# One transformer block after another on one core: which instructions rank first on three engines, and the recurrence's functions ordered by kind

## The chip, the cores and the metric

The kernel runs on one core of a Trainium2 chip. A core has a tensor engine (TensorE, PE in the profile) that multiplies 128 x 128 weights with up to 512 columns and writes to PSUM, a vector engine (DVE), a scalar engine with table functions (ACT), GpSimd (POOL, which here reads and writes SBUF only), and a sync engine (SP) that only issues transfers here. Each engine works off its own queue in order, and a semaphore holds an instruction back until its inputs are there. The metric is the device time in microseconds (us): 2860.61 is the median of three runs (2860.28 to 2860.99).

## The reference

512 tokens of width 1024, fp32, go through two blocks.

The first block (depth 1): a hybrid mixer (dilated attention of 8 heads and a retention of 4 heads on the normalised input, joined by an output projection), cross attention to 256 memory tokens (4 heads), and a SwiGLU feed-forward with 2816 hidden columns. Each of the three is added as `x + rms_norm(y)`.

The second block (depth 2), each layer: half a SwiGLU feed-forward, a mixer, half a SwiGLU feed-forward, each with a shift, a scale and a gate worked out from a conditioning vector `c` by a 1024 x 9216 matrix. Its mixer joins a gated linear recurrence on 512 channels, stick-breaking attention (4 heads) and forgetting attention (4 heads):

```
r, i  = sigmoid(u @ w_r + b_r), sigmoid(u @ w_i + b_i)
a     = exp(-8 * r * softplus(-lam))
h_t   = a_t * h_(t-1) + sqrt(1 - a_t^2) * i_t * u_t
y_lru = h * gelu(lru_g)
y     = concat(rms(y_lru), rms(y_sb), rms(y_fox)) * g_mix_out
x     = x + gate * (y @ w_out)
```

## The kernel before, in words

**Matrix products.** Every large product runs as three products of split numbers (`mm3`, L367 to L373): an fp32 weight tile of 128 x 1024 is loaded by SP (`weights`, L339, three raw buffers), ACT casts it to the upper half (L348), DVE, or in a few places POOL, subtracts to get the lower half (L350), with six buffers for each half. Activations are kept as such pairs too. The token axis of 512 is the column axis.

**Stage ends.** A stage that ends in a norm is cut into two halves of 256 tokens (`slab4` with `halves`, L431). For each of 8 row tiles and each half, DVE adds the PSUM result into X (`end_plain`, L571) or into Y (`end_post`, L599), ACT squares it and POOL sums the squares (`square_sum`, L514 to L524). A product with ones sums over partitions (`cols`, L485), `rsqrt` (L472) scales on DVE (L475) and takes the power -0.5 on POOL (L476), and `spread` turns the result back into a row for all partitions (L508). From that, DVE, ACT and POOL make the next activations (`norm_half`, L540 to L561). In the first block, `end_post` with `apart` squares and sums the new X as well (L628). The weights for the next stage are loaded and split beforehand (L451 to L453).

**The feed-forward** (`ffn`, L666) works in three slabs of 9, 9 and 4 hidden tiles, gate and up first and then down; the end of the third slab is the stage end above.

**The conditioning products** (`ada`, L837): 144 rows, each a 512 KB transfer through the raw buffers and one DVE multiply-and-sum (L849). While `calm` is true, each call of `weights` adds 0.7 row to what is due (L341); stage ends set `calm` to false, the first gate-up products to true (L400). `modulated(n)` calls for what is still missing.

**The second block's mixer** (`mixer2`, L1393): q and k of the stick-breaking heads; then values by tokens (`keep`, L1620), copied out of PSUM by ACT and DVE in turn (`copy`, L334); q and k of the forgetting heads (`qk`, L1419); then the recurrence's inputs (`lru_in`, L1633). Meanwhile the heads run as streams: scores, exponentials, turning the probabilities over TensorE into PSUM (`flip`), a copy to SBUF (`turn`, L1503), and the product with the values (`weigh`, L1508). `lru` (L1325) holds the recurrence: tanh for the gates, exponential, square root, scan, gelu, then squares and sums. The output projection's first half (`ev`, L1650) adds to X while the recurrence ends.

**What sets the order.** TensorE's order is written out by hand: streams (`Flow`, L214) yield their planned time or a `Wait`, and the table `T` (L193) has the planned delays, such as the gap between a sum of squares and the broadcast of 1/rms (L505) or the gap after the recurrence (`lru_sum`, L1388). ACT, DVE, POOL and SP are ordered by the framework: it plays the program with its own estimate of times, and of the instructions that are ready on an engine takes the one with the lowest priority number, which is the order of writing. `issue_after(x)` puts instructions behind x in their engine's queue, without a wait for its end. ACT's functions lie in table sets; where the next function is not in the set that is loaded, a table load is put in.

Of the kernel before, what the change touches and what calls it, by code (L numbers as in the profile page):

```python
# [13 lines left out]
AF = mybir.ActivationFunctionType  # L14
# [171 lines left out]
def _pe(n, passes=4):  # L186
# [6 lines left out]
T = dict(early0=4, early1=4, fox_tail=1.09, fox=1.0, plain0=2.6, post0=2.25, plain1=4.41,  # L193
         post1=4.2, dil_tail=1.5, dil_end=5.0, dil_turn=2.3, rsqrt=3.51, norm=0.6, post=0.38,
         apart=8.0, squares=4.73, rope=10.0, rope_k=6.24, ret=4.0, ret_e=2.0, ret_gn=8.0, aq=4.0,
# [95 lines left out]
class Core:  # L291
# [37 lines left out]
    def vec(self, name, j=0, n=1):  # L329
        o, w = VEC[name]  # L330
        assert j + n <= w
        return self.V[:, o + j:o + j + n]

    def copy(self, i, out, src):  # L334
# [137 lines left out]
    def rsqrt(self, src, n, scale, eps):  # L472
        nc = self.nc
        m, y = (self.tiny(q, n) for q in ("rs_m", "rs_y"))
        nc.vector.tensor_scalar(m, src, scale, eps, op0=OP.mult, op1=OP.add)  # L475
        nc.gpsimd.tensor_tensor(y, m, self.power[:, :n], op=OP.pow)  # L476
        return y
# [86 lines left out]
    def end_plain(self, srcs, X, gate, nxt, H, made=None):  # L564

        nc = self.nc
        sums = []

        def evac(m, ps, o, n):
            x = self.X[m][:, o:o + n]  # L570
            nc.vector.scalar_tensor_tensor(x, ps, gate(m), x, op0=OP.mult, op1=OP.add)  # L571
            if nxt:
                self.square_sum(sums, x, self.half, m)
            else:
                nc.sync.dma_start(self.out[o // 256, m], x)

        def norm(hf, accs):
            bc = []
            yield from self.spread(accs, 2, 1.0 / D, bc)
            yield from self.norm_half(hf, bc[0], nxt[0], nxt[1], H)  # L580

        def half(hf):
            if nxt:
                H.made[hf] = self.flow.spawn(norm(hf, list(sums)), T[f"plain{hf}"])
                sums.clear()
        if nxt:
            H += self.new_h()
        yield from self.slab4(srcs, X, evac, half, made=made)

    def end_post(self, srcs, X, Y, gpost, nxt, H, apart=None, made=None):  # L590
# [6 lines left out]
        def evac(m, ps, o, n):  # L597
            y = Y[m][:, o:o + n]
            nc.vector.tensor_tensor(y, ps, y, op=OP.add)  # L599
            self.square_sum(sums, y, self.half, (o == 0 or m % 4) if apart else m)  # L600

# [64 lines left out]
    def ffn(self, gu, dn, H, acc_evac, end):  # L666
# [23 lines left out]
        c = 0  # L690
        for s, (k0, n) in enumerate(SLABS):
            yield from self.dense_t([gu[2 * k0 + i] for i in range(2 * n)], H, evac(k0), 0 if s else 5)
            self.calm = self.calm and s < 2
            if n == 4:
# [58 lines left out]
    def setup(self):  # L753
# [3 lines left out]
        self.V = self.cp.tile([128, NV], F32, name="V")  # L757
        nc.scalar.dma_start(self.V, I["vec"])
        self.X0 = X0
        self.ident = self.cp.tile([128, 128], F32, name="ident")  # L760
# [564 lines left out]
    def lru(self, l, LX, LG, HL, opened):  # L1325
# [10 lines left out]
        for m in range(4):  # L1336
# [13 lines left out]

            nc.scalar.activation(g, r, AF.Tanh, scale=a4[:, m:m + 1], bias=a4[:, m:m + 1])  # L1351
            U.append(u), R.append(r), G.append(g)
        bd.clear()
        for m in range(4):
            c = a4[:, 4 + m:5 + m]
            nc.scalar.activation(R[m], R[m], AF.Exp, scale=c, bias=c)
        for m in range(4):
# [5 lines left out]
        for m in range(4):  # L1363
            u, a, g = U[m], R[m], G[m]
            nc.scalar.activation(g, g, AF.Sqrt, scale=0.25)  # L1365
            nc.gpsimd.tensor_tensor(u, u, g, op=OP.mult)

            nc.vector.tensor_tensor_scan(g, a, u, 0.0, op0=OP.mult, op1=OP.add)
# [3 lines left out]
        for m in range(4):  # L1372
            nc.scalar.activation(LG[m], LG[m], AF.Gelu_apprx_tanh)
            nc.vector.tensor_tensor(U[m], G[m], LG[m], op=OP.mult)
            self.square_sum(sums, U[m], self.rot)
        HL += [(self.act("lh", F32R), self.act("ll", F32R)) for _ in range(4)]

        def norm(hf):
            sl, out = slice(hf * 256, hf * 256 + 256), []
            yield from self.spread([sums[0][:, sl]], 2, 1.0 / 512, out)  # L1380
            for m in range(4):
# [11 lines left out]
    def mixer2(self, l, H, H2):  # L1393
# [25 lines left out]
        def qk(t, ps):  # L1419
            o, sq = self.act("fqk"), self.rot("fsq")  # L1420
            fqk[t] = o
            nc.scalar.activation(o, ps, AF.Copy)
            nc.scalar.activation(sq, o, AF.Square)
# [75 lines left out]
        def turn(e, h, t):  # L1499
            n = t * 128 + 128  # L1500
            pt = self.flip([e[:, j * 128:j * 128 + 128] for j in range(t + 1)])
            pT = self.rot("pT2")
            self.copy(h, pT[:, :n], pt)  # L1503
            return pT
# [115 lines left out]
        def keep(t, ps):  # L1620
            v[t] = self.act("v2")
            self.copy(t, v[t], ps)
        yield from self.dense_tok([I["m_v"][l, c] for c in range(4)], H, keep, e=nc.gpsimd)
# [9 lines left out]
        def lru_in(i, ps):  # L1633
# [8 lines left out]
            else:  # L1642
                LG[i - 4] = self.act("lgg")
                self.copy(i, LG[i - 4], ps)
        lru = flow.spawn(self.lru(l, LX, LG, HL, opened), 1.0)
# [4 lines left out]
        def ev(m, ps, o, n):  # L1650
            nc.vector.scalar_tensor_tensor(self.X[m], ps, gate(m), self.X[m], op0=OP.mult, op1=OP.add)
        yield from _joined(sticks + foxes)
# [95 lines left out]
```

## Time and profile before

| | |
|---|---|
| median of 3 runs | 2860.61 us |
| profiled execution | 2859.76 us, span of its instructions 2858.0 us |
| TensorE busy | 2773.4 us, 97% |
| TensorE loading weights | 2355.9 us, 82% |
| DVE, ACT, POOL busy | 1448.9, 1044.9, 422.2 us (51, 37, 15%) |
| mean granted clock of TensorE | 0.984 of full speed |
| HBM traffic | 113 GB/s over the span |

Times of rows are microseconds from the start of the span, single durations of groups are nanoseconds. A line such as L336 can be a helper's, called from several places. A matmul counts as busy from its start to its modelled end, so 97% does not say that TensorE works at its peak. What stands in brackets at the end of a row is the idle time before it and who ended it.

### The profile page before, as it was taken

The page shows a single profiled execution, that of the slowest core. Times are in us where ns is not written, and L with a number is a line of the kernel's source. Part 1 is how long each engine was busy: PE and PEld are TensorE (multiplying, and loading weights), DVE is VectorE, ACT ScalarE, POOL GpSimd, SP SyncE. Part 2 cuts the span into 40 slices and gives each one's busy share as a digit, 9 for nine tenths or more (in the row PEclk, how much of TensorE's full clock was granted, in tenths as well). Part 3 has the DMA queues.
Part 4 walks back from the last instruction along what each step waited for, and adds up shares of the span by engine and source line. Part 5 has one row for each costly group of instructions (what it writes and reads, how often), then busy time and mean ns, then how long its engine had stood idle before and what let it go on. Part 6 is the DMA issues. An engine that isn't in the chain of part 4 may idle for free. (4 is left out here: it accounts for less than half of the span.)

```text
span 2858.0 us, 36557 instructions
## 1 busy us (share of the span) xinstructions
PE 2773.4 (97%) x14536; PEld 2355.9 (82%) x14536; DVE 1448.9 (51%) x2421; ACT 1044.9 (37%) x1753; POOL 422.2 (15%) x415
## 2 busy tenths in 40 slices
PE   8999999999999999998989999999999989999999
PEld 7888878888888888897778888898888877888888
DVE  5365656545455444446565455464333565743333
ACT  4355444323233222245464222242222455632221
POOL 4020314101031000043231000020000331400000
PEclk9999999999998999999999999999999989999999
DMA  5322422555533555421125555354333211232322
GB/s 166 122 70 83 132 68 89 168 159 165 156 119 109 156 169 162 128 73 52 60 65 164 162 171 158 107 170 155 111 96 96 67 59 60 67 96 89 104 94 69
DMA packets 94602, 326.03 MB, mean 114 GB/s; under 512 B 11232, under 2 KB 15584, under 8 KB 94432
## 3 DMA queue, kind: packets, MB, share of 16 engines
q1 hardware_dynamic: 94288, 323.53, 36.2%
q8 instruction: 114, 1.87, 0.3%
q14 instruction: 56, 0.46, 0.1%
q10 hardware_dynamic: 144, 0.18, 0.0%
HBM read 321.37 MB, written 2.10 MB: 113 GB/s over the span
## 5 line engine op out<-in xcount | busy, mean ns | idle before, releaser
L348 ACT ACTIVATE wh<-wr 128x1024 fp32r<-128x1024 f32 x450 | 475.8, 1059 | 1269.0 <-PE mm L371 532.0
L370 PE MATMUL mm<-hh,wh 128*128 128x512 f32 (+1 forms) x2248 | 835.5, 372 | 0.8 <-DVE X L571 0.8
L371 PE MATMUL mm<-hl,wh 128*128 128x512 f32 (+1 forms) x2248 | 822.8, 366 | 1.9 <-DVE hl L532 1.9
L372 PE MATMUL mm<-hh,wl 128*128 128x512 f32 (+1 forms) x2248 | 822.4, 366 | 0.8 <-DVE wl L350 0.8
L350 DVE TENSOR_TENSOR wl<-wr,wh 128x1024 fp32r<-128x1024 f32 x434 | 538.4, 1244 | 327.6 <-ACT wh L348 323.3
L371 PEld LDWEIGHTS mm<-hl,wh 128*128 128x128 f32 x2248 | 427.3, 190 | 71.2 <-issue 3.6
L370 PEld LDWEIGHTS mm<-hh,wh 128*128 128x128 f32 x2248 | 427.3, 190 | 70.9 <-issue 3.6
L372 PEld LDWEIGHTS mm<-hh,wl 128*128 128x128 f32 x2248 | 427.0, 190 | 69.4 <-DVE wl L350 1.2
L849 DVE CUSTOM_DVE_ANT_0 ada<-ada,c 128x1024 f32<-128x1024 f32 x144 | 180.5, 1254 | 336.3 <-DMA ada<-in_w_ada_dram 336.1
L371 PE MATMUL dn<-ul,wh 128*128 128x512 f32 x720 | 280.2, 389 | 0.2 <-DVE ul L687 0.2
L370 PE MATMUL dn<-uh,wh 128*128 128x512 f32 x720 | 280.1, 389 | 0.0
L372 PE MATMUL dn<-uh,wl 128*128 128x512 f32 x720 | 280.1, 389 | 0.0
L522 POOL TENSOR_TENSOR acc<-sq,sq 128x256 f32<-128x256 f32 (+1 forms) x29 | 31.6, 1089 | 1179.1 <-ACT sq L519 1087.2
L684 DVE TENSOR_TENSOR sg<-mm,sg 128x512 f32<-128x512 f32 x110 | 75.9, 690 | 192.7 <-PE mm L372 187.9
L370 PE MATMUL mmt<-wh,hh 128*128 128x512 f32 x352 | 145.5, 413 | 18.0 <-ACT v L336 9.9
L371 PEld LDWEIGHTS dn<-ul,wh 128*128 128x128 f32 x720 | 135.1, 188 | 28.7 <-DVE ul L687 0.7
L372 PEld LDWEIGHTS dn<-uh,wl 128*128 128x128 f32 x720 | 135.1, 188 | 28.1
L370 PEld LDWEIGHTS dn<-uh,wh 128*128 128x128 f32 x720 | 135.1, 188 | 28.0
L371 PE MATMUL mmt<-wl,hh 128*128 128x512 f32 x352 | 140.7, 400 | 0.5 <-DVE wl L350 0.5
L372 PE MATMUL mmt<-wh,hl 128*128 128x512 f32 x352 | 140.4, 399 | 0.0
L522 POOL TENSOR_TENSOR acc<-acc,sq 128x256 f32<-128x256 f32 (+1 forms) x134 | 119.4, 891 | 65.4 <-ACT sq L519 57.1
L721 DVE SCALAR_TENSOR_TENSOR X<-dn,gate,X 128x512 f32<-128x512 f32 x64 | 47.9, 749 | 136.6 <-PE dn L372 136.6
(335 smaller groups left out, 3726.9 us busy)
## 6 DMA issues: line engine op xcount, KB each, us to landing
wr<-in_f_gu_dram SPq DMA_DIRECT2D x176, 512.0 KB, 3.6
ada<-in_w_ada_dram SPq DMA_DIRECT2D x144, 512.0 KB, 4.2
wr<-in_f_dn_dram SPq DMA_DIRECT2D x88, 512.0 KB, 3.5
wr<-in_w_gu_dram SPq DMA_DIRECT2D x44, 512.0 KB, 3.5
wr<-in_w_in_dram SPq DMA_DIRECT2D x28, 512.0 KB, 3.6
wr<-in_m_t_dram SPq DMA_DIRECT2D x24, 512.0 KB, 3.5
wr<-in_w_dn_dram SPq DMA_DIRECT2D x22, 512.0 KB, 3.6
wr<-in_m_v_dram SPq DMA_DIRECT2D x16, 512.0 KB, 3.6
```

The costliest lines, as they stand in the source:

```text
L348: nc.scalar.activation(hi, raw, AF.Copy)
L350: (e or nc.vector).tensor_tensor(lo, raw, hi.bitcast(F32), op=OP.subtract)
L370: mm(ps, ah, bh, start=start, stop=False)
L371: mm(ps, ah, bl, start=False, stop=False)
L372: mm(ps, al, bh, start=False, stop=stop)
L522: nc.gpsimd.tensor_tensor(acc, accs.pop(), sq, op=OP.add)
L684: nc.vector.tensor_tensor(t, ps, t, op=OP.mult)
L721: self.nc.vector.scalar_tensor_tensor(self.X[m], ps, gate(m), self.X[m], op0=OP.mult, op1=OP.add)
L849: nc.vector.tensor_tensor_reduce(out=w, in0=w, in1=c, scale=1.0, scalar=0.0, op0=OP.mult, op1=OP.add, accum_out=ml[:, i:i + 1])
```

## The change

`hot()` gives the framework's priority 0, the start of the program, to the instructions inside, so that they are taken first of all that are ready on their engine. It is put around `rsqrt`, the additions and square sums of `end_plain` and `end_post`, the copy of q and k of the forgetting heads (which now alternates between ACT and DVE), the copy of the turned probabilities, the copies of the values and of the recurrence's gate, and the addition of the mixer's output projection. The planned gap of 1/rms goes from 3.51 to 2.0. `calm` turns false before the third gate-up slab instead of after it. A table set (number 18, which has silu) is loaded in `setup`. In `lru`, ACT's exponentials are queued behind the last tanh, the square roots behind the last exponential, and the gelus behind the last square root; the last of four squares is summed by TensorE instead of POOL.

```diff
@@ -191,7 +191,7 @@
 
 
 T = dict(early0=4, early1=4, fox_tail=1.09, fox=1.0, plain0=2.6, post0=2.25, plain1=4.41,
-         post1=4.2, dil_tail=1.5, dil_end=5.0, dil_turn=2.3, rsqrt=3.51, norm=0.6, post=0.38,
+         post1=4.2, dil_tail=1.5, dil_end=5.0, dil_turn=2.3, rsqrt=2.0, norm=0.6, post=0.38,
          apart=8.0, squares=4.73, rope=10.0, rope_k=6.24, ret=4.0, ret_e=2.0, ret_gn=8.0, aq=4.0,
          ak=4.0, dil=2.0, mem=8.0, dil_1=0.11, dil_2=0.5, mem_e=6.32, mem_p=2.24, mem_q=1.5,
          lru_tanh=2.88, lru_sum=25.0, lru_end=2.52, fqk=8.0, gate_f=24.0, gate_s=0.6, finish=4.91,
@@ -330,6 +330,10 @@
         o, w = VEC[name]
         assert j + n <= w
         return self.V[:, o + j:o + j + n]
+
+    def hot(self):
+
+        return self.tc.high_priority()
 
     def copy(self, i, out, src):
 
@@ -472,8 +476,9 @@
     def rsqrt(self, src, n, scale, eps):
         nc = self.nc
         m, y = (self.tiny(q, n) for q in ("rs_m", "rs_y"))
-        nc.vector.tensor_scalar(m, src, scale, eps, op0=OP.mult, op1=OP.add)
-        nc.gpsimd.tensor_tensor(y, m, self.power[:, :n], op=OP.pow)
+        with self.hot():
+            nc.vector.tensor_scalar(m, src, scale, eps, op0=OP.mult, op1=OP.add)
+            nc.gpsimd.tensor_tensor(y, m, self.power[:, :n], op=OP.pow)
         return y
 
     def cols(self, accs, ncol, scale, out):
@@ -568,10 +573,11 @@
 
         def evac(m, ps, o, n):
             x = self.X[m][:, o:o + n]
-            nc.vector.scalar_tensor_tensor(x, ps, gate(m), x, op0=OP.mult, op1=OP.add)
-            if nxt:
-                self.square_sum(sums, x, self.half, m)
-            else:
+            with self.hot():
+                nc.vector.scalar_tensor_tensor(x, ps, gate(m), x, op0=OP.mult, op1=OP.add)
+                if nxt:
+                    self.square_sum(sums, x, self.half, m)
+            if not nxt:
                 nc.sync.dma_start(self.out[o // 256, m], x)
 
         def norm(hf, accs):
@@ -596,8 +602,9 @@
 
         def evac(m, ps, o, n):
             y = Y[m][:, o:o + n]
-            nc.vector.tensor_tensor(y, ps, y, op=OP.add)
-            self.square_sum(sums, y, self.half, (o == 0 or m % 4) if apart else m)
+            with self.hot():
+                nc.vector.tensor_tensor(y, ps, y, op=OP.add)
+                self.square_sum(sums, y, self.half, (o == 0 or m % 4) if apart else m)
 
         def norm(hf, accs):
             sl = slice(hf * 256, hf * 256 + 256)
@@ -689,8 +696,8 @@
             return f
         c = 0
         for s, (k0, n) in enumerate(SLABS):
+            self.calm = self.calm and s < 2
             yield from self.dense_t([gu[2 * k0 + i] for i in range(2 * n)], H, evac(k0), 0 if s else 5)
-            self.calm = self.calm and s < 2
             if n == 4:
                 break
             w9 = self.weights(dn[c])
@@ -756,6 +763,8 @@
         self.X = [X0[:, m] for m in range(NK)]
         self.V = self.cp.tile([128, NV], F32, name="V")
         nc.scalar.dma_start(self.V, I["vec"])
+
+        self.load_table(18)
         self.X0 = X0
         self.ident = self.cp.tile([128, 128], F32, name="ident")
         nc.gpsimd.memset(self.ident, 1.0)
@@ -1348,12 +1357,14 @@
                 yield Wait(0.3)
             nc.vector.scalar_tensor_tensor(u, g, 1.0, u, op0=OP.add, op1=OP.mult)
 
-            nc.scalar.activation(g, r, AF.Tanh, scale=a4[:, m:m + 1], bias=a4[:, m:m + 1])
+            last = nc.scalar.activation(g, r, AF.Tanh, scale=a4[:, m:m + 1], bias=a4[:, m:m + 1])
             U.append(u), R.append(r), G.append(g)
         bd.clear()
-        for m in range(4):
-            c = a4[:, 4 + m:5 + m]
-            nc.scalar.activation(R[m], R[m], AF.Exp, scale=c, bias=c)
+
+        with self.tc.issue_after(last.ins):
+            for m in range(4):
+                c = a4[:, 4 + m:5 + m]
+                last = nc.scalar.activation(R[m], R[m], AF.Exp, scale=c, bias=c)
         for m in range(4):
             u, a, g = U[m], R[m], G[m]
 
@@ -1362,7 +1373,8 @@
             nc.vector.scalar_tensor_tensor(g, q, 1.0, g, op0=OP.add, op1=OP.mult)
         for m in range(4):
             u, a, g = U[m], R[m], G[m]
-            nc.scalar.activation(g, g, AF.Sqrt, scale=0.25)
+            with self.tc.issue_after(last.ins):
+                root = nc.scalar.activation(g, g, AF.Sqrt, scale=0.25)
             nc.gpsimd.tensor_tensor(u, u, g, op=OP.mult)
 
             nc.vector.tensor_tensor_scan(g, a, u, 0.0, op0=OP.mult, op1=OP.add)
@@ -1370,14 +1382,16 @@
             yield Wait(0.5)
         sums = []
         for m in range(4):
-            nc.scalar.activation(LG[m], LG[m], AF.Gelu_apprx_tanh)
+            with self.tc.issue_after(root.ins):
+                nc.scalar.activation(LG[m], LG[m], AF.Gelu_apprx_tanh)
             nc.vector.tensor_tensor(U[m], G[m], LG[m], op=OP.mult)
-            self.square_sum(sums, U[m], self.rot)
+
+            self.square_sum(sums, U[m], self.rot, m < 3)
         HL += [(self.act("lh", F32R), self.act("ll", F32R)) for _ in range(4)]
 
         def norm(hf):
             sl, out = slice(hf * 256, hf * 256 + 256), []
-            yield from self.spread([sums[0][:, sl]], 2, 1.0 / 512, out)
+            yield from self.spread([sq[:, sl] for sq in sums], 2, 1.0 / 512, out)
             for m in range(4):
                 t = self.half("ln")
                 nc.vector.scalar_tensor_tensor(t, U[m][:, sl], self.vec(f"g_mix{l}", m), out[0],
@@ -1419,7 +1433,8 @@
         def qk(t, ps):
             o, sq = self.act("fqk"), self.rot("fsq")
             fqk[t] = o
-            nc.scalar.activation(o, ps, AF.Copy)
+            with self.hot():
+                self.copy(t, o, ps)
             nc.scalar.activation(sq, o, AF.Square)
             if t % 2 == 0:
                 squares[t] = self.tiny("fss", 16)
@@ -1500,7 +1515,8 @@
             n = t * 128 + 128
             pt = self.flip([e[:, j * 128:j * 128 + 128] for j in range(t + 1)])
             pT = self.rot("pT2")
-            self.copy(h, pT[:, :n], pt)
+            with self.hot():
+                self.copy(h, pT[:, :n], pt)
             return pT
 
         def weigh(pT, h, t, O, v0):
@@ -1619,7 +1635,8 @@
 
         def keep(t, ps):
             v[t] = self.act("v2")
-            self.copy(t, v[t], ps)
+            with self.hot():
+                self.copy(t, v[t], ps)
         yield from self.dense_tok([I["m_v"][l, c] for c in range(4)], H, keep, e=nc.gpsimd)
         yield from self.dense_tok([I["m_v"][l, 4 + c] for c in range(4)], H, qk)
         turned = flow.spawn(self.turn(fqk, "fT", FT, scaled), T["fqk"])
@@ -1641,14 +1658,17 @@
                 LX[i] = u
             else:
                 LG[i - 4] = self.act("lgg")
-                self.copy(i, LG[i - 4], ps)
+                with self.hot():
+                    self.copy(i, LG[i - 4], ps)
         lru = flow.spawn(self.lru(l, LX, LG, HL, opened), 1.0)
         yield from self.dense_t([I["m_t"][l, i] for i in range(8)], H, lru_in)
         H.clear()
         gate = self.gate2(l, 1)
 
         def ev(m, ps, o, n):
-            nc.vector.scalar_tensor_tensor(self.X[m], ps, gate(m), self.X[m], op0=OP.mult, op1=OP.add)
+            with self.hot():
+                nc.vector.scalar_tensor_tensor(self.X[m], ps, gate(m), self.X[m], op0=OP.mult,
+                                               op1=OP.add)
         yield from _joined(sticks + foxes)
         yield from _joined(list(ends.values()))
         yield from self.slab4(I["m_o"][l, 1], [YT[k] for k in range(4)], ev, e=nc.gpsimd)
```

## Rows read from the trace of the kernel before

**Rows 1.** Page, part 1: busy us, share of the span, instructions.

```profile
PE 2773.4 (97%) x14536; PEld 2355.9 (82%) x14536; DVE 1448.9 (51%) x2421; ACT 1044.9 (37%) x1753; POOL 422.2 (15%) x415
```

**Rows 2.** Windows, TensorE: from:to, us, PE busy, PEclk, DMA share, GB/s.

```profile
835.00:885.00 50.00, 41.13 (x280) 0.76 0.25 76
1290.00:1306.00 16.00, 11.05 (x51) 0.79 0.32 98
1323.00:1347.00 24.00, 18.11 (x109) 0.86 0.07 23
1347.00:1425.00 78.00, 71.75 (x409) 0.98 0.20 61
1440.00:1480.00 40.00, 32.84 (x153) 0.87 0.20 66
2440.00:2470.00 30.00, 23.25 (x110) 0.89 0.29 88
```

**Rows 3.** Waits of TensorE: us in total, times, longest us.

```profile
PE ms L485 <- POOL acc L522: 16.0, 7, 4.5
PE bc L508 <- POOL rs_y L476: 11.5, 5, 5.2
PE mmt L370 <- ACT v L336: 9.9, 2, 5.0
...
PE tp L736 <- ACT fe L1554: 5.8, 6, 1.8
PE SO L1508 <- ACT pT L336: 5.7, 2, 2.8
PE SO L1508 <- DVE pT L336: 5.4, 4, 1.8
...
PE S L1492 <- DVE pT L336: 3.1, 1, 3.1
PE sl L370 <- DVE X L1651: 2.2, 2, 1.1
PE mm L371 <- DVE hl L532: 1.9, 3, 1.0
```

**Rows 4.** Timeline, 1297 to 1299, ACT and TensorE: start us, us, what.

```profile
1297.75 0.63 ACT L1597 ACTIVATE z<-z 128x512 f32<-128x512 f32 x1 [2.47 <-POOL z L1596]
...
1298.90 0.80 PE L370 MATMUL mmt<-wh,hh 128*128 128x512 f32 x1 [4.95 <-ACT v L336]
```

**Rows 5.** Timeline, 1463 to 1469, DVE and TensorE.

```profile
1463.30 0.50 PE L485 MATMUL ms<-ones,acc 128*128 128x1 f32 x4
...
1467.88 0.15 DVE L475 TENSOR_SCALAR rs_m<-ms 128x2 f32<-128x2 f32 x1
...
1468.87 1.22 PE L508 MATMUL bc<-ident,rs_y 128*128 128x128 f32 x4 [5.07 <-POOL rs_y L476]
```

**Rows 6.** Timeline, 845 to 854, DVE and TensorE.

```profile
845.44 3.63 PE L494 MATMUL ms<-ones,sq 128*128 128x1 f32 x32
...
847.39 1.41 DVE L599 TENSOR_TENSOR y<-slh,y 128x256 f32<-128x256 f32 x4
...
853.21 1.01 PE L485 MATMUL ms<-ones,acc 128*128 128x1 f32 x4 [4.14 <-POOL acc L522]
```

**Rows 7.** Timeline, 346 to 352, POOL.

```profile
346.34 5.25 POOL L522 TENSOR_TENSOR acc<-acc,sq 128x256 f32<-128x256 f32 x5
```

**Rows 8.** Groups of instructions by line, ACT's table loads: busy us, mean ns.

```profile
L1365 ACT ACT_TABLE_LOAD x6 | 7.7, 1283 | 0.1
```

**Rows 9.** Timeline, 1226 to 1230, POOL and TensorE.

```profile
1226.05 0.72 POOL L476 TENSOR_TENSOR rs_y<-rs_m,power 128x2 f32<-128x2 f32 x1 [1.94 <-DVE rs_m L475]
...
1229.67 0.60 PE L508 MATMUL bc<-ident,rs_y 128*128 128x128 f32 x4
```

**Rows 10.** Timeline, 0 to 7, ACT.

```profile
5.27 1.28 ACT L531 ACT_TABLE_LOAD   x1 [5.27 <-DMA X<-in_x_dram]
```

**Rows 11.** Windows, all engines: us, PE, PEld, DVE, ACT, POOL busy, PEclk.

```profile
2000.00:2100.00 100.00, 100.00 (x443) 82.81 (x442) 36.37 (x43) 27.80 (x34) 0.00 (x0) 1.00 0.35 106
```

## The prediction

> **What bounds the kernel now.** I read the page's busy line first [rows 1]: TensorE is busy 2773.4 us of 2858.0, the vector engine (DVE) half of it, the scalar engine (ACT) and GpSimd (POOL) less. So only what TensorE waits for, and the clock it is granted, can move the time: 2858.0 - 2773.4 = 84.6 us of idle time. Second, windows around the places where TensorE is short of work [rows 2]: the reader is to take width minus busy time as idle, and (1 - PEclk) times the width as lost to the lower of the two clock levels (1.2 instead of 2.4 GHz), where TensorE was busy then. That gives, idle + clock, in us:
> - end of the first feed-forward (C, 835-885) 8.9 + 12.0
> - second block's mixer, layer 0: values (E1, 1290-1306) 5.0 + 3.4, stick-breaking attention (E2, 1323-1347) 5.9 + 3.4, forgetting attention (E3, 1347-1425) 6.3 + 1.6, recurrence's end (F, 1440-1480) 7.2 + 5.2; layer 1 repeats this, F there with 6.8 + 3.3.
>
> Third, the list of TensorE's waits [rows 3], which names who ended each. Fourth, the order of work just before the long ones [rows 4 to 7]. The pattern is one: the awaited instruction is short, its input is ready, and it stands in its engine's queue behind something that TensorE does not need yet. In E1 the copy of the values out of PSUM sits on ACT behind an exponential that itself waited 2.47 us for POOL [rows 4]. In F the sum of squares is issued at 1463.30, over at 1463.80, and the 0.15 us instruction on it starts at 1467.88 [rows 5]. In C the last four PSUM additions run at 847.39 in one go, though TensorE had turned to its next work at 845.44 [rows 6].
>
> **The change part by part.**
>
> *Copy of the values first (L1623).* Both layers: 9.9 us in 2 waits [rows 3]. The copy goes to ACT's head when its PSUM is ready, which is before TensorE stops; the 4.95 us go, and about 2.5 of the 3.4 us of clock around them (the rest lies under the idle time itself). 7.5 us a layer, 15 in all.
>
> *Copies of the turned probabilities first (L1503).* Waits for pT: 5.7 + 5.4 + 3.1 = 14.2 us over both layers [rows 3], and E2's clock loss of 3.4 us a layer, of which I take 2: 18 in all.
>
> These 33 us are gross. While TensorE stood still in E1, the stick-breaking heads' exponentials went on; with TensorE earlier, they and the scans before them are late next, and the waits for the forgetting attention's exponential (L1554, not promoted), 5.8 us [rows 3], stay. I keep 70%: 23 us. Bounds: 0 (all given back) to 37 (the idle 9.9 + 14.2 and 13 of clock).
>
> *1/rms first (L475, L476).* The waits of bc for rs_y are 11.5 us in 5 [rows 3]; F has two of them, 5.07 [rows 5] and its like in layer 1 (longest 5.2). The scaling came 1467.88 - 1463.80 = 4.08 us after its sum, so each falls by some 4.0, 8.0 together. The promoted additions of the mixer's output (L1651) take most of the 2.2 us of waits of sl (2), and of F's clock loss of 5.2 + 3.3 I take half, 4. Sum 14; bounds 0 to 19.
>
> *Planned gap of 1/rms from 3.51 to 2.0.* The broadcast matmuls move 1.51 us forward in TensorE's order at every sum. In a clean passage the result is there at 1226.05 + 0.72 = 1226.77 and the broadcast starts at 1229.67 [rows 9]: 2.9 us of slack, of which 1.4 remain. So no cost, while POOL and DVE answer promptly; behind a POOL sum of 1.05 us [rows 7] the slack is nearly used up. Bounds: -10 (25 halves gain 0.4 each in the next stage) to +40 (25 halves wait 1.6 each). I take 0, nearest to the clean rows.
>
> *Additions, squares and their sums at stage ends first (L571, L599, L519, L522).* C: with the additions at their arrival instead of 847.39, the sums run up to 3 us earlier and TensorE's wait of 4.14 [rows 6] goes, while the other half's normalisation moves back by 4 additions of 0.35, 1.4 us: net some 3. One row of the conditioning vector (1.2 us of DVE) also leaves this stretch by the moved `calm` line, and 1 us of clock goes: 5 in all. Bounds 0 to 15. The 1.5 us waits for sums at the end of the second block's first feed-forward in each layer (part of the 16.0 in rows 3) are of the same kind; half of them come back as waits for lower halves on POOL, so 1.5. At the ends of the first mixer and of the cross attention TensorE waits for POOL's sums over the new X, five in a row [rows 7], which L628 issues outside the promoted blocks: I take 0, with 3 to either side (promoted work ahead of them delays them, the earlier start helps).
>
> *The recurrence kind by kind (L1351 to L1373).* 20 table loads stand at these lines and L1554, of 1283 ns each, 6 of them at L1365 [rows 8]; ordered by kind there are 3 a layer, so 14 go, 14 x 1.28 = 18 us of ACT. But TensorE's order puts the sum a planned 25 us after the recurrence, and it met no wait there [rows 5]. So 0 on the path; it is the cover that lets F keep its gain. What stands behind the new order: the exponentials wait in ACT's queue for the last tanh, and behind them weight casts (L348) and the outputs' scaling. The last sum is no longer added on POOL but by TensorE, 2 more small matmuls a half: under 0.5 us.
>
> *PSUM copies of the recurrence's gate and of q, k (L1644, L1422).* Half of L1422 moves to DVE; no wait in rows 3 is theirs: 0.
>
> *The conditioning vector.* 8 weights x 0.7 rows x 4 feed-forwards = 22 rows (a 512 KB DMA on SP's queue and 1.2 us of DVE each) move to later gate-up stretches, the last to 2000-2200, where DVE is busy 36% [rows 11]: 0. One or two rows fall into layer 1's mixer end; without cover some 5 us.
>
> *Table load at the start.* ACT stands until 5.27 for x and then loads a table for 1.28 us [rows 10] ahead of its first casts; before x it is free. TensorE's start moves by 1.2 us.
>
> Sum: 23 + 14 + 5 + 1.5 + 1.2 = 44.7, some 45 us. The profiled execution took 2859.76 (span 2858.0 and 1.8 around it), 0.85 below the median of 2860.61. 2859.8 - 45 = 2814.8, as a median about 2816.
>
> **The rivals.**
>
> *Given back in the mixer.* ACT, DVE and POOL hand the attention's exponentials to each other [rows 4], and this may be the true bound: the 23 us turn into waits of the turning matmuls for z or fe. Against it: waits that copies of PSUM end add up to 9.9 + 14.2 us [rows 3], and a copy needs nothing but its PSUM. Then only 14 + 5 + 1.5 + 1.2 = 22 us are won: 2839. Chance 0.20.
>
> *Promoted sums starve the next stage (the slower side).* At ten half ends of the plain kind, seven POOL sums go ahead of the lower halves of the next activations, and DVE's additions ahead of weight splits. At 1.05 us a sum [rows 7] that is 7 us a half. If half of it, 3.5 us, becomes TensorE's wait for hl or wl, with 2.5 us of lower clock behind it as in E1, it costs 10 x 6 = 60 us, and the kernel ends at 2816 + 60 = 2876. It decides the sign from 45 / 10 = 4.5 us a half on. Against it: the waits of mm for hl are 1.9 us in all [rows 3], so there is room. Chance 0.08.
>
> The Trainium skill (SBUF — State Buffer, Who interferes with whom) says that a DVE instruction with two SBUF inputs and a GpSimd instruction that reads SBUF shut each other out for the whole instruction, the later one blocked. By that rule promoted sums would also lengthen the weight splits they meet, which speaks for this rival. The 1.05 us a sum in rows 7 are in line with it; it would add one sum's length to a split.
>
> *The order hardly moves.* Priority decides only between instructions that the framework's own clock holds ready together; where it does not, the copies stay where they are. Then the start, C's row and little else count: 4 us, 2857. Chance 0.05.
>
> *Nearly all goes.* The upper bounds, 37 + 19 + 15 + 3 + 1.3 = 75 us: 2786. Chance 0.12.
>
> **How the numbers follow.** The forecast has the remaining 0.55. Range 2790 to 2850: the forecast (its own, 2800 to 2832), the given-back case and the near part of the full one. 0.2%, 5.7 us, is about what a measurement of this kernel can tell from no change. Faster by more: 0.55 + 0.20 + 0.12 = 0.87; within: 0.05; slower by more: 0.08.
>
> **What would show it.** E1 without a wait of mmt for v, and the clock at 1.00 there; waits of SO and S for pT below 5 us of 14; bc for rs_y near 2 us of 11.5; at C the additions done by 846 and the wait of ms below 1 us; three table loads a layer in the recurrence; POOL's sums over the new X waited for as before. Wrong: new waits of mm for hl or wl above 10 us, of bc for rs_y above 15, or of the turning matmuls for z and fe that make up for those for pT.

## The result and the profile after

The changed kernel takes 2885.46 us (median of four runs, 2884.28 to 2894.20) against 2860.80 beside it: a ratio of 1.0092 (95% interval 1.0072 to 1.0112), 21 to 32 us slower. The forecast was 2816. The profiled execution is the one of 2894.20, some 9 us above the other three; where these 9 lie one trace can't tell, so places are taken from the experiments' traces as well.

TensorE's busy line, after, answering [rows 1]:

```profile
PE 2789.1 (96%) x14552; PEld 2372.6 (82%) x14552; DVE 1459.2 (50%) x2425; ACT 1026.4 (35%) x1734; POOL 429.0 (15%) x413
```

Idle time grew from 84.6 to 2892.2 - 2789.1 = 103.1 us. Busy time grew by 15.7 for the same products and 16 small ones: the mean granted clock fell from 0.984 to 0.978 (0.006 x 2892 = 17). ACT lost 18.5 us of work, nearly all of it 15 table loads of 1.28, and the time did not follow. TensorE's waits, after (us in total, times, longest), answering [rows 3]:

```profile
PE ms L490 <- POOL acc L527: 22.9, 7, 7.5
PE bc L513 <- POOL rs_y L481: 12.2, 4, 4.3
...
PE sl L374 <- DVE X L1670: 7.0, 4, 3.0
PE S L1507 <- DVE fT L1457: 6.2, 2, 3.1
PE tp L743 <- ACT fe L1570: 5.8, 6, 1.8
PE mmt L374 <- ACT av L904: 5.5, 1, 5.5
PE SO L1524 <- DVE pT L340: 4.0, 2, 2.0
PE mmt L374 <- ACT v L340: 3.7, 2, 1.9
PE SO L1524 <- ACT pT L340: 3.4, 2, 1.7
```

The waits for v and pT that were to go did shrink (9.9 to 3.7; 14.2 to some 7.4). But sums are waited for longer (16.0 to 22.9), 1/rms as long as before, and there are waits that were not there or small: av 5.5, fT 6.2 (1.0), the output projection's X 7.0 (2.2).

Where TensorE falls behind can be read from matmuls that both kernels issue at the same point, the sums over partitions (start in us; the last column is the run e2 below, the kernel before with the planned gap alone changed; its first sum, at 27.23, is 0.5 us earlier than before):

| sum at | before | after | gap alone |
|---|---|---|---|
| memory tokens | 179.15 | 179.20 | 178.68 |
| end of first mixer | 325.62 | 333.61 (+8.0) | 332.63 (+7.0) |
| end of cross attention | 460.32 | 473.50 (+13.2) | 475.43 (+15.1) |
| end of first feed-forward | 835.83 | 855.62 (+19.8) | 856.56 (+20.7) |
| second block, first half feed-forward | 1225.27 | 1242.86 (+17.6) | 1244.53 (+19.3) |
| recurrence, layer 0 | 1463.30 | 1485.82 (+22.5) | 1482.71 (+19.4) |
| same feed-forward, layer 1 | 2220.02 | 2242.68 (+22.7) | 2240.02 (+20.0) |
| recurrence, layer 1 | 2456.78 | 2489.07 (+32.3) | 2475.51 (+18.7) |

So 18 to 20 us are lost in the first block, as many as the planned gap loses there alone, and the rest in the second block's mixers, in this trace most of it in layer 1's. The first loss, in windows of TensorE (from:to, us, busy of PE, PEld, DVE, ACT and POOL, clock), before and then after:

```profile
180.00:200.00 20.00, 20.00 (x108) 16.74 (x108) 16.34 (x75) 10.93 (x26) 2.46 (x8) 1.00 0.29 90
```

```profile
180.00:200.00 20.00, 14.53 (x54) 11.45 (x53) 14.04 (x65) 6.55 (x13) 2.46 (x8) 0.83 0.13 37
```

5.47 us idle and 0.17 x 20 = 3.4 us of clock. What TensorE waits for there is the copy of the first mixer's values, av. ACT before, then ACT and TensorE after:

```profile
181.89 1.37 ACT L895 ACTIVATE av<-mmt,rs 128x512 f32<-128x512 f32 x2 [4.19 <-PE mmt L372]
```

```profile
183.64 1.20 ACT L1178 ACTIVATE mh<-mn 128x256 fp32r<-128x256 f32 x3 [5.55 <-DVE mn L1176]
185.92 1.20 ACT L1178 ACTIVATE mh<-mn 128x256 fp32r<-128x256 f32 x3 [1.07 <-DVE mn L1176]
188.16 0.42 ACT L1178 ACTIVATE mh<-mn 128x256 fp32r<-128x256 f32 x1 [1.04 <-DVE mn L1176]
188.48 0.67 ACT L904 ACTIVATE av<-mmt,rs 128x512 f32<-128x512 f32 x1
...
189.20 0.80 PE L374 MATMUL mmt<-wh,hh 128*128 128x512 f32 x1 [5.47 <-ACT av L904]
```

ACT stands idle for 5.55 us and still has the copy behind seven halves of the memory's split, which wait for the broadcast. The copy's input was there at 181.9; its place in the queue was not. In the kernel before it stood ahead of them.

### The profile page after: what moved, and what is told of

Read it like the earlier page. It is cut to its first block, busy times and chain, and to the rows that moved or that the text cites. A ratio compares the mean times of both kernels' runs of the same rounds, so it can differ in the third digit from the quotient of the medians.

```text
span 2892.2 us, 36577 instructions
## 1 busy us (share of the span) xinstructions
PE 2789.1 (96%) x14552; PEld 2372.6 (82%) x14552; DVE 1459.2 (50%) x2425; ACT 1026.4 (35%) x1734; POOL 429.0 (15%) x413
## 5 line engine op out<-in xcount | busy, mean ns | idle before, releaser
L527 POOL TENSOR_TENSOR acc<-acc,sq 128x256 f32<-128x256 f32 x132 | 120.6, 915 | 46.4 <-ACT sq L524 35.8
```

The source lines that it names most:

```text
L527: nc.gpsimd.tensor_tensor(acc, accs.pop(), sq, op=OP.add)
```

## The experiments

Every kernel ran in five rounds beside the kernel before (medians 2857.5 to 2859.6); "us" below is ratio minus 1, times that median, with the 95% interval in brackets.

### e1 to e4: planned gap and promotions, apart

e1: everything as changed, but

```
-rsqrt=2.0
+rsqrt=3.51
```

> The changed kernel with the planned gap of 1/rms back at 3.51; all else as changed. Theory 1 (the loss is TensorE's written order, pulled forward at every 1/rms by the shorter planned gap: 8 us at the memory values near 190, 5 at the end of the first mixer, 8 at the end of cross attention, 4 behind it): these 25 us go, 2885 - 25 = 2860, and TensorE's wait of 5.5 us for av and the wait of 6.9 us for a sum near 495 are gone. Theory 2 (the promoted instructions are the loss): the time stays, 2880 to 2888, and the waits stay. Theory 3 (the recurrence ordered by kind is the loss, 4 to 8 us in each layer): 2880 or above too, with its waits at the mixers' ends unchanged.

1.0051 (+15, 10 to 19). The wait for av is gone, and no sum of POOL's is waited for longer than 2.2 us. Theory 1 holds for its places, but 15 us remain that it does not explain. In this trace TensorE's idle time is back at 2870.8 - 2786.2 = 84.6 us; what remains is busy time (2786.2; 2773.4 before), at a mean granted clock of 0.981.

e2: the kernel before with `rsqrt=2.0`, nothing else.

> The kernel before with only the planned gap of 1/rms shortened to 2.0. Theory 1 (planned gap): slower by about 25 us, 2886, with the wait for av near 190 and longer waits for sums at the ends of the first mixer and of cross attention. Theories 2 (promotion) and 3 (recurrence): no change, 2858 to 2864.

1.0080 (+23, 18 to 27). One number makes most of the loss, and in the table above all of it arises before 860. Theories 2 and 3 can't give this. Here the loss is idle time, 2877.8 - 2773.5 = 104.3 us (84.6 before), and busy time is as before.

e3: everything as changed, but `hot()` returns an empty context.

> The changed kernel with nothing promoted (each instruction has the priority of its place in the program); planned gap 2.0, recurrence by kind, the conditioning rows and the table load as changed. Theory 1 (planned gap): the promotions' gain at the values (some 4 us in layer 0) is lost and the gap's loss stays: 2885 to 2893. Theory 2 (promotion): the loss goes, 2858 to 2864. Theory 3 (recurrence): 2870 to 2876, the promotions' part gone and the recurrence's left.

1.0101 (+29, 24 to 34): theory 1's range. At the short gap the promotions cost nothing: with them TensorE is 2.4 us earlier at the sum that ends the first block (855.62; 858.07 in e3) and 4.3 us later at the last recurrence's (2489.07; 2484.73).

e4: e3 with `rsqrt=3.51`.

> As the run before this one, and the planned gap back at 3.51: what is left of the change is the recurrence by kind with its last square summed by TensorE, the alternating copy of q and k, the moved conditioning rows and the early table load. Theory 1 (planned gap): 2858 to 2864. Theory 2 (promotion): the same 2858 to 2864. Theory 3 (recurrence): 2870 to 2876, with TensorE's new waits for X at the output projection (3.0 and 0.5 us) still there.

1.0033 (+9, 6 to 12). Neither theory 1 nor 2 allowed this. Theory 3's size fits at its low end (its range was 9 to 15 us above the 2860.8 beside the changed kernel), and its waits of sl for X are there, 9.6 us in two. Whether these make the 9 us is asked next.

### e5: the recurrence by kind alone

The `lru` hunks of the diff on the kernel before.

> The kernel before with the recurrence's functions ordered by kind, and the last of its four squares summed by TensorE; nothing promoted, planned gap 3.51. Theory 3 (this order costs: the four scans then stand in one row on DVE, ahead of the output projection's additions): slower by 6 to 10 us, 2864 to 2868, with TensorE's waits of sl for X at 9 to 10 us (2.2 before) and of bc for rs_y at 4 to 5 us (11.5 before). Rival, my forecast (off the path, only cover): 2856 to 2861, the waits for X at 2 us.

1.0023 (+7, 4 to 9). DVE, POOL and TensorE of this run, layer 0:

```profile
1447.94 0.74 DVE L1654 SCALAR_TENSOR_TENSOR X<-sl,gate,X 128x512 f32<-128x512 f32 x1
1448.60 7.11 DVE L1370 TENSOR_TENSOR_SCAN li<-lr,lx 128x512 f32<-128x512 f32 x4
1455.63 1.86 DVE L1377 TENSOR_TENSOR lx<-li,lgg 128x512 f32<-128x512 f32 x3
1457.42 0.74 DVE L1654 SCALAR_TENSOR_TENSOR X<-sl,gate,X 128x512 f32<-128x512 f32 x1
...
1445.73 7.78 POOL L1368 TENSOR_TENSOR lx<-lx,li 128x512 f32<-128x512 f32 x4
...
1458.21 0.79 PE L370 MATMUL sl<-yh,wh 128*128 128x512 f32 x1 [4.78 <-DVE X L1654]
```

Before, the scans began at 1443.81, 1447.88, 1452.40 and 1454.73, with table loads between the square roots of the first three, and additions of the output projection came between them. By kind, the four scans run back to back and no PSUM tile is released for 9.5 us; TensorE stops for 4.78.

So the stop is as theory 3 has it, but it does not make the 7 us. The waits of sl for X grew by 7.4 us (9.6; 2.2 before), and those of bc for rs_y fell by 6.2 (5.3; 11.5), as I had hoped of another part. TensorE's idle time in this trace is 2864.1 - 2779.6 = 84.5 us, with 84.6 before. The span grew by busy time, and part of that is a lower clock in a place that the edit does not touch, ahead of layer 1's recurrence and behind the same wait of 4.94 us for v. Page of e5, then a window of TensorE in e5 and before:

```profile
PE 2779.6 (97%) x14552; PEld 2361.8 (82%) x14552; DVE 1455.1 (51%) x2421; ACT 1027.9 (36%) x1739; POOL 424.6 (15%) x413
...
2306.00:2316.00 10.00, 10.00 (x64) 0.77 0.01 2
...
2306.00:2316.00 10.00, 10.00 (x87) 1.00 0.01 2
```

Why the order by kind costs 7 us over twelve runs stays open.

### e6, e11, e14: values and turned probabilities

e6:

```
+            with self.hot():
                 self.copy(t, v[t], ps)          # keep
...
+            with self.hot():
                 self.copy(h, pT[:, :n], pt)     # turn
```

> The kernel before with only the copies of the values and of the turned probabilities promoted. My forecast for this part (the copies are late because of their place in the queue): faster by 23 us, 2834. Rival (given back inside the mixer: the wait for v falls from 5.0 to 1.9 us and those for pT from 8.6 to 3.7 a layer, and waits for the decays, the lower halves and fT take their place before 1370): within 3 us of before, 2854 to 2861, and TensorE's first scores of the forgetting heads at 1369 to 1371 as before (1369.6).

1.0020 (+6, 3 to 9). Worse than the rival: the waits for v fall from 9.9 to 3.7 us, but those for fT rise from 1.0 to 6.2, of S for pT from 3.1 to 7.5, and for the decays ab from 0 to 2.6. TensorE meets the forgetting heads' first scores when it did before (1369.63). TensorE and DVE of e6:

```profile
1366.31 1.21 DVE L354 TENSOR_TENSOR wl<-wr,wh 128x1024 fp32r<-128x1024 f32 x1
1367.44 1.52 DVE L1645 SCALAR_TENSOR_TENSOR lx<-mm,V,lx 128x511 f32<-128x511 f32 x2
1368.88 0.74 DVE L1446 TENSOR_SCALAR fT<-tp,V 128x512 f32<-128x512 f32 x1
...
1369.77 1.13 PE L1496 MATMUL S<-fT,fT 64*128 64x512 f32 x4 [3.11 <-DVE fT L1446]
```

fT is late for its place in a queue again: behind a weight split and two convolution steps. e11 promotes it too:

```
+            with self.hot():
                 if p < 2: ...                    # scaled(): the copies fT
```

> The kernel with the copies of the values and of the turned probabilities promoted (2864.5), and the scaled copies fT of the turned q and k of the forgetting heads promoted as well. If their place in DVE's queue alone ends the stretch (the copy at 1368.9 stands behind a weight split and two convolution steps): the wait of S for fT falls from 3.1 to 1 us in each layer and the time by 4 to 8 us, 2856 to 2861. If the stretch is bound by the chain behind it (1/rms of q and k, turning, scores, exponentials): TensorE's next waits grow by as much and the time stays at 2862 to 2867.

1.0022 (+6, 4 to 9), and the wait stays at 3.1 us: the promoted copies passed a single convolution step. DVE of e11:

```profile
1366.07 1.22 DVE L354 TENSOR_TENSOR wl<-wr,wh 128x1024 fp32r<-128x1024 f32 x1
1367.20 1.53 DVE L1646 SCALAR_TENSOR_TENSOR lx<-mm,V,lx 128x511 f32<-128x511 f32 x2
1368.64 1.40 DVE L1447 TENSOR_SCALAR fT<-tp,V 128x512 f32<-128x512 f32 x2
1369.96 0.74 DVE L1646 SCALAR_TENSOR_TENSOR lx<-mm,V,lx 128x509 f32<-128x509 f32 x1
```

e14 takes the copies off that queue instead:

```
-                nc.vector.tensor_scalar(o, ps, self.vec(f"g_k{l}"), None, op0=OP.mult)
+                nc.scalar.activation(o, ps, AF.Copy, scale=self.vec(f"g_k{l}"))
```

> The kernel with the copies of the values and of the turned probabilities promoted (2864.5), and all four scaled copies fT of a layer on ACT, which stands idle there for 5 us, instead of two on DVE behind a weight split and two convolution steps. If the queue on DVE bounds the stretch: TensorE's wait of S for fT falls from 3.1 to under 1 us in each layer and the time by 4 to 6 us, 2858 to 2861. If the chain behind it (scores, exponentials) bounds it: the wait goes, and waits of the turning matmuls for fe grow from 5.8 us by as much; 2862 to 2867.

1.0001 (+0, -2 to +3): 5 to 6 us better than e6, with the scores at 1368.07 and a wait of 0.6. So the queue did hold the stretch. But the waits for fe rise from 5.8 to 7.5 us and the gain over the kernel before is still nothing.

### e7: 1/rms and the output projection's additions

`hot()` in `rsqrt` and in `ev` alone.

> The kernel before with only 1/rms and the additions of the mixer's output projection promoted. My forecast for this part: faster by 14 us, 2843, with the waits of bc for rs_y at 3 to 4 us (11.5 before). Rival (the additions, taken first, push the recurrence's scans back, so the last sum is late by as much): within 4 us of before, with a new wait of ms for sq or acc near 1463.

1.0015 (+4, 2 to 7). The wait that was to go is longer, 5.86 us ([rows 5] had 5.07). TensorE, ACT and DVE of e7:

```profile
1459.83 0.60 PE L490 MATMUL ms<-ones,acc 128*128 128x1 f32 x4 [0.25 <-POOL acc L527]
1466.30 1.22 PE L513 MATMUL bc<-ident,rs_y 128*128 128x128 f32 x4 [5.86 <-POOL rs_y L481]
...
1462.41 1.06 ACT L352 ACTIVATE wh<-wr 128x1024 fp32r<-128x1024 f32 x1 [4.18 <-DMA wr<-in_f_gu_dram]
...
1463.50 1.23 DVE L354 TENSOR_TENSOR wl<-wr,wh 128x1024 fp32r<-128x1024 f32 x1 [0.84 <-ACT wh L352]
1464.65 0.74 DVE L1657 SCALAR_TENSOR_TENSOR X<-sl,gate,X 128x512 f32<-128x512 f32 x1
1465.31 0.15 DVE L480 TENSOR_SCALAR rs_m<-ms 128x2 f32<-128x2 f32 x1
```

The sum is over at 1460.4, and rs_m still stands behind a weight split that waits for a cast, which waits 4.18 us for its transfer, and behind a promoted addition. The rival's wait of ms did not come (0.25); the part failed for a third reason. That explains why nothing was won. The 4 us of loss are not in this trace, whose span (2857.6) is that of before; the mean granted clock of the twelve runs is 0.982, with 0.984 before.

### e8: the stage ends

`hot()` in `end_plain` and `end_post` alone.

> The kernel before with only the additions, squares and sums at the stage ends promoted. My forecast for this part: faster by 6.5 us, 2851. Rival (promoted sums starve the next stage): slower by 5 to 10 us, 2863 to 2868: at each half end TensorE's first product of the next stage waits 1 to 3 us for hl, with POOL's sums in front of the lower halves, 10 to 11 us of such waits in all (1.9 before).

0.9996 (-1, -4 to +1): neither time, but the rival's waits came, 10.4 us of mm for hl (1.9 before). Against them, TensorE gains at the first block's ends: the sum that opens the second block comes 6 us earlier (1219.32; 1225.27 before). At the second block's ends POOL's lower halves are late, at two half ends, not ten: 5.4 us in two waits. One of them, TensorE and POOL:

```profile
1233.67 0.58 PE L375 MATMUL mm<-hl,wh 128*128 128x256 f32 x1 [2.69 <-POOL hl L561]
...
1229.69 2.38 POOL L354 TENSOR_TENSOR wl<-wr,wh 128x1024 fp32r<-128x1024 f32 x1 [1.10 <-ACT wh L352]
1232.02 0.91 POOL L526 TENSOR_TENSOR acc<-acc,sq 128x256 f32<-128x256 f32 x1
1232.89 0.72 POOL L561 TENSOR_TENSOR hl<-hn,hh 128x256 fp32r<-128x256 f32 x1
```

The promoted sum is 0.91 us of it. In front of both stands a weight split on POOL, which before came behind the lower half at this place (1235.64 and 1234.90).

### e9, e12, e13: where the gap costs

Gap 2.0 at one place each: the memory's 1/rms (`spread(sums, ..., gap=2.0)`); the whole second block; the 1/rms of Y at the first block's three ends.

> The kernel before with one planned gap of 27 shortened to 2.0: that of the memory tokens' 1/rms, near 180. Theory 1 (the gap does its harm through the order of writing: seven splits of the memory then stand ahead of the copies of av in ACT's queue, and TensorE waits 5.5 us for these with a stretch at the lower clock behind it): slower by 8 us, 2867, all of it between 180 and 200. Rival (the gap costs in many small waits over the whole kernel): within 2 us of before.

> The kernel before with the planned gap of 1/rms shortened to 2.0 in the second block alone, where the clean passages lie from which I took my price of nothing. Theory 1 (the gap's 23 us lie in the first block): 0 to 4 us slower, 2859 to 2863. Rival (it costs at every half end): some 10 us slower, 2869.

> The kernel before with the planned gap shortened to 2.0 at six of the 27 places alone: the 1/rms of Y at the three stage ends of the first block. Theory 1 (order of writing: the squares and sums of the new X of the first half are then written, and queued on ACT and POOL, ahead of the last squares of Y's second half): slower by 9 to 12 us, 2867 to 2870, with waits of ms for POOL's sums of 7 us at the ends of the first mixer and of cross attention (3.8 and 4.5 before). Rival (the loss at these ends in the run with all gaps short was a late effect of the stall near 190): within 2 us of before.

Measured: e9 1.0041 (+12, 8 to 16), e12 1.0014 (+4, 1 to 6), e13 1.0042 (+12, 7 to 17). The sum, 28, fits e2's 18 to 27 within these intervals; the rivals fall. These are 21 of the 25 gaps; the other four, in the first block, were not moved alone. In e9 one gap of 25 is moved (27 above is a miscount), the order in ACT's queue is that of the kernel after, and TensorE waits 5.46 us for av. (Its profiled execution is 6.6 us behind at the sum that ends the first block and 1.5 at the last mixer's end; its median is 10 us above that of before. So the trace shows the loss near 190, but not that it reaches the end.) e13 shows the stage ends; TensorE, DVE, ACT and POOL at the end of cross attention:

```profile
492.20 1.44 PE L485 MATMUL ms<-ones,acc 128*128 128x1 f32 x6 [7.27 <-POOL acc L522]
...
482.15 0.42 DVE L599 TENSOR_TENSOR y<-slh,y 128x256 f32<-128x256 f32 x1
...
488.24 0.42 ACT L519 ACTIVATE sq<-y 128x256 f32<-128x256 f32 x1 [0.44 <-POOL acc L522]
...
485.64 6.51 POOL L522 TENSOR_TENSOR acc<-acc,sq 128x256 f32<-128x256 f32 x6
```

The last addition into Y is done at 482.6, its square comes at 488.24, when POOL's sums of the other half's new X have given a buffer back, and its own sum ends POOL's row of six. Before, the last square followed its addition (473.04) at 473.57.

### e10, e15: a version faster than both

e10: the early `load_table(18)` and `hot()` in `end_post` alone.

> The kernel before with two parts of the change only: the early table load, and the additions, squares and sums at the three stage ends of the first block promoted. If the gain of 8 us by 900 that the run with all stage ends promoted showed is that of the first block's ends, and its loss after 1215 that of the second block's: 9 us faster than before, 2850, faster than both kernels. Rival (TensorE's later start of each stage, not the place of the promotion, gives the gain back): within 2 us of before.

2854.25 us, 0.9986 (0.9975 to 0.9997), -4 us (-7 to -1): faster than both kernels, at under half of the expected 9.

e15: e10 with `hot()` in `rsqrt`.

> The version with the early table load and the first block's stage ends promoted (2854.3, 3.6 below before in its runs), with 1/rms promoted as well. If 1/rms is held by its rank: 4 to 8 us faster than before by that part, some 2848. If it is held by the weight split in front of it, which waits for a transfer that the framework expects earlier: the waits of bc for rs_y stay at 12 us, 2853 to 2856.

0.9994 (-2, -5 to +1): no gain. The waits of bc for rs_y are 10.6 us in 4 (12.6 in e10), so rank does little; the second account holds. In this trace the first block's gain is gone as well: the sum that ends it comes at 835.88 (830.47 in e10, 835.83 before).

## Why the prediction was wrong

**The steps that failed** are two. The first is the gain of the promotions: nearly all of the 44.7 us were to come from instructions taken first, 23 of them from the copies of the values and of the turned probabilities. As a whole they gained nothing: the promotions cost some 6 us at the long gap (e1 less e4). Without the short gap the change still costs 15 us (e1), outside the forecast's range. The parts below say what came instead.

The second is "planned gap of 1/rms from 3.51 to 2.0", priced at 0. It cost 23 us, inside its own bounds (-10 to +40); alone it would have left the forecast at 2839, inside the range. The rows were right: in the second block the slack of 2.9 us in [rows 9] is real, and e12's 4 us are small for its 14 gaps. But I asked only whether TensorE would stand waiting for 1/rms, and bounded the loss by 25 halves of such waits. The harm was elsewhere, in two places of the first block that [rows 9] say nothing of. A planned gap moves when the following instructions are written; on ACT, DVE and POOL that is their rank. So the memory's split went ahead of av, and squares of the new X ahead of the last squares of Y. I had said of POOL that its slack there "is nearly used up" [rows 7], and then priced by the clean row.

The kernel came out on the slower side, which had a chance of 0.08, but not by the mechanism that I gave for it: waits of mm for hl are 1.6 us after (1.9 before). They came only where the gap was 3.51 (11.7 us in e1, 10.4 in e8), and there they did not cost the 60 us.

**Values and turned probabilities, 23 us.** The rival "given back in the mixer" won, and was too kind: +6. My markers were half right (the waits of SO and S for pT did not fall below 5 in e6: 15.6 with 14.2 before). The reason I gave against the rival, that a copy needs nothing but its PSUM, was true and beside the point: the next copy, fT, also needed only its PSUM and stood in a queue too.

**1/rms and additions in F, 14 us.** It cost 4. In [rows 5] I read an instruction held by its rank. It was held by a weight split that the queue already had ahead of it and that waited for a transfer. The rival "the order hardly moves" had this mechanism, with a chance of 0.05 and for all places at once.

**Recurrence by kind, 0 on the path.** +7. The table loads went (15 left of 30, where I counted 14 gone). I looked for what waits behind the exponentials on ACT and not at DVE, where the scans lost the gaps into which additions fell. In waits that is nearly paid back by 1/rms; the 7 us are busy time in e5's trace, and their cause is open.

**Stage ends, 6.5 us.** About 1 (-1 to +4). In e8's trace the ends of the first mixer and of cross attention gain 3.8 us (832.06; 835.83 before), where I took 0, and C 2.2, where I took 5; the second block's ends give it back.

**Start, 1.2 us.** Nothing. TensorE's first sum comes at 27.80 (27.73 before); in runs with the early load it lies at 26.37 to 27.80, in runs without it at 26.66 to 28.01. The cast of x starts 1.25 us earlier (5.32 instead of 6.57), but two squares then go ahead of the first weight cast, which gains 0.23 us (6.75; 6.98).

The parts add to 23 + 7 + 6 + 4 - 1 = 39; the whole costs 26. They are not independent: all promotions together cost some 6 us at the long gap (e1 less e4) and gain some 3 at the short one (the whole less e3), neither far clear of the intervals. That promoted squares are worth more where the short gap makes them late would fit this; no run shows it. The remainder of e4 over e5, 3 us, is within the two intervals; what the moved conditioning rows cost stays open.

## What to carry to other kernels

A planned delay in a hand-written order is also a rank for every other engine that is ordered by when an instruction is written: price it by who changes places in each queue, not by the slack of the engine that waits. A priority acts at the moment at which a planner holds instructions ready; where the queue was late on the chip for another reason (a transfer, a split in front), it changed next to nothing (e7, e11), and moving the instruction to an idle engine did (e14), though not the time of the whole. Table loads on an engine off the path were here the gaps that let another engine's additions through (e5). Take idle and busy time apart before a loss is put down to a wait: the gap's loss was idle time, the rest of this change's was busy time.

## What the runs showed of the hardware

DVE and POOL lengthened each other once the recurrence ran by kind. Groups by line of the kernel after (busy us, mean ns), scans and the products that feed them; then POOL and DVE of e5, layer 0, where two products and two scans meet:

```profile
L1378 POOL TENSOR_TENSOR lx<-lx,li 128x512 f32<-128x512 f32 x8 | 15.6, 1979 | 0.0
L1380 DVE TENSOR_TENSOR_SCAN li<-lr,lx 128x512 f32<-128x512 f32 x8 | 14.2, 1838 | 0.0
...
1449.13 4.38 POOL L1368 TENSOR_TENSOR lx<-lx,li 128x512 f32<-128x512 f32 x2
...
1450.17 4.42 DVE L1370 TENSOR_TENSOR_SCAN li<-lr,lx 128x512 f32<-128x512 f32 x2
```

Before, the same 16 instructions took 1338 and 1489 ns on the mean; where nothing ran beside them a product took 1.29 us and a scan 1.21. The Trainium skill (SBUF — State Buffer, Who interferes with whom) has a DVE instruction with two SBUF inputs and a GpSimd instruction that reads SBUF contend. The trace agrees that they do: 2.2 us each in the rows of e5. In the 4.38 us of the two products DVE did some 2.2 scans, an estimate from the share of each scan's time that lies in them. One behind the other these would take 2 x 1.29 + 2.2 x 1.21 = 5.2 us, so they overlap in part.
